# Order of VectorE's work in a two-layer encoder: gate sums held behind a split, spread additions, placed low parts, reordered row blocks

## The chip, the cores and the metric

The kernel runs on one core of a Trainium2 chip. The metric is the time on the device of one execution, in microseconds (us). The kernel is one program that goes through the whole model once. The five engines are called as in the profile: PE (TensorE, matmuls), PEld (its weight loads), DVE (VectorE), ACT (ScalarE), POOL (GpSimd), and SP (SyncE), which issues most of the DMA transfers. Each engine works through a list of instructions in a fixed order that is set when the program is built; an instruction starts when the one before it on its engine is done and the semaphores that it waits for have arrived.

## What is computed

The reference is an encoder of two layers on a sequence of 1024 rows of 1024 numbers, all float32. The first layer mixes by latent attention, the second by differential attention; both are chunk-causal.

```
for i in range(DEPTH):                       # 2 layers
    mix = mla(h) if i % 2 == 0 else diff(h)
    h = layernorm(ALPHA * h + mix, ...)
    h = layernorm(ALPHA * h + swiglu(h, w_gu[i], w_down[i]), ...)

swiglu(x) = (silu(gate) * up) @ w_down,      gate, up = split(x @ w_gu)
```

x is (1024, 1024), w_gu is (1024, 2 x 2816) and w_down is (2816, 1024). The change concerns only swiglu and the layer norm behind it (in the second layer).

## The kernel before

**Products of 2x2 blocks by seven.** Both matrix products of swiglu are done with seven block products instead of eight: sums and differences of blocks of the activations and of the weights are formed first, seven products ("1" to "7") are taken, and their results are added up. In the gate stage, a unit (n, pr) is product pr for block n of 22 weight blocks. Its weight side comes from `prepare` (line 573) and its matmuls from `consume` (line 602). The activation side is the operands t1, t2, t3, t4 and b22.

**Two parts for every operand.** PE multiplies in fp32r, so `split` (line 509) cuts every operand into a high part (an ACT cast) and a low part (a subtraction on DVE or POOL, line 511); a product then is three matmuls per 128 rows: high by high, high by low, low by high. One unit of the gate stage is 12 matmuls of 128x512. Tiles called op_* hold both parts of an operand.

**Gate stage.** Six weight blocks are begun ahead (`load_pre`): their products "1" and "2" run while the layer norm ahead still ends. Each load_pre takes a buffer tagged wr, of which there are two, for the raw weights gp, so that the load of gp n + 2 can be issued when the subtractions that read gp n are done. The raw blocks gr of the other units come in by load (line 564), and a gate sum (line 586, then 588 and 590) forms sums and differences in place in gr. The raw loads are 1 MB each for gr and 512 KB for gp, all on SP's queue.

**Down stage.** Four accumulators of one PSUM bank each serve one product, `whole` (line 865), 4 banks by 11 parts of the contraction. An activation part op_h comes from `from_h`, a weight part from a generator such as `t1` or `t4`. When a product is done, `added` (line 881) adds its four banks to rows of z on DVE, and the banks can be used again. The first product's 12 additions (line 921) stand in the program between it and the second. The last product of the last layer ("4") runs part by part on all four banks for parts 0 and 1, then on two banks for parts 2 to 10, then on the other two; its weight parts are called wt41_j, with low parts on POOL for j = 0 and 1 and on DVE for the others.

**What sets the order.** The program is written as a stream of operations; the build sorts them by priority and dependency into one order for each engine. `behind(i, j)` (line 167) adds a dependency without a semaphore between instructions, so that i is kept after j in that order. banks_read, h_lows and t4_lows are lists of instructions kept for that purpose: the additions that read banks, the low parts of the activation parts, and those of the last product's weight parts.

**The tail.** Behind the last product each of four row blocks goes through add (line 987), centred (998), scale (1003, with a power on POOL in 1004) and done (1009, followed by its store from SP in 1010). `on_v` chains these DVE instructions in written order.

## Time and profile before

| | us |
|---|---|
| median of 3 runs (lowest, highest) | 2276.8 (2276.53, 2277.06) |
| profiled execution | 2275.05 |
| its span, first to last instruction | 2273.3 |
| PE busy in the span | 2245.0 |
| DVE, ACT, POOL busy | 1550.6, 1016.7, 862.6 |
| mean granted clock of PE, share of full speed | 0.998 |

The profiled execution is 1.75 us longer than its span. Rows of the timeline read: start, length, engine, line, operation, output<-inputs, size, number of like instructions in a row, and in brackets the idle time of the engine before it with what ended it. Lengths of DVE instructions in a row overlap a little: the starts of 128x512 subtractions follow each other by 0.60 us, though each is listed with 0.68. Line numbers are those of the kernel before. Two names: the first number behind a tile's name is the layer (0 or 1), the last one counts buffers and can be passed over.

### The profile page before, as it was taken

Reading aid. Unit: us, or ns where it says so; the run is one execution under the profiler, and the core shown is the slowest. Engines: PE = TensorE matmul, PEld = TensorE weight load, DVE = VectorE, ACT = ScalarE, POOL = GpSimd, SP = SyncE. Lnnn points to the kernel's source line nnn. Section 1 sums busy time; section 2 is a strip of 40 time slices with the busy share of each in tenths; the row PEclk is TensorE's granted clock in tenths of the full one; section 3 lists DMA queues with packets and bytes.
Section 4 is the critical chain, followed back from the end, with each engine's and each line's share of the span. In section 5 each row is a group of like instructions: output and inputs, shape, how many; then the busy total and the mean of one; then the engine's idle time right before and its main releaser. Section 6 shows DMA issues by size and latency. Waiting matters only on the chain. (4 is left out here: it accounts for less than half of the span.)

```text
span 2273.3 us, 31157 instructions
## 1 busy us (share of the span) xinstructions
PE 2245.0 (99%) x11426; PEld 1914.2 (84%) x11426; DVE 1550.6 (68%) x2909; ACT 1016.7 (45%) x2101; POOL 862.6 (38%) x673
## 2 busy tenths in 40 slices
PE   9999999999999999999999999999999999999998
PEld 9898998888888888888888898987778888888886
DVE  6666665596656668778476667576587666668778
ACT  4465664352333334445465656555442333334443
POOL 2233452114444446555232424221014444446562
PEclk9999999999999999999999999999999999999999
DMA  5121325334313238554310212153344223247554
GB/s 206 41 97 59 119 98 186 139 140 140 126 70 139 70 126 323 196 179 167 107 47 23 67 38 70 26 208 116 125 153 152 94 98 111 96 156 271 181 179 149
DMA packets 104281, 289.33 MB, mean 127 GB/s; under 512 B 8640, under 2 KB 31808, under 8 KB 93632
## 3 DMA queue, kind: packets, MB, share of 16 engines
q1 hardware_dynamic: 100128, 277.90, 34.8%
q0 software_dynamic: 4000, 9.44, 1.5%
q8 instruction: 90, 1.47, 0.3%
q14 instruction: 63, 0.52, 0.1%
HBM read 205.78 MB, written 77.33 MB: 125 GB/s over the span
## 5 line engine op out<-in xcount | busy, mean ns | idle before, releaser
L511 ACT CAST op_g<-gr 128x512 fp32r<-128x512 f32 x240 | 147.5, 622 | 404.7 <-PE gb L555 225.2
L511 POOL TENSOR_TENSOR op_g<-gr,op_g 128x512 fp32r<-128x512 f32 x104 | 146.0, 1408 | 300.6 <-DVE tmp L649 160.5
L511 DVE TENSOR_TENSOR op_h<-rh,op_h 128x512 fp32r<-128x512 f32 x154 | 163.7, 1092 | 61.2 <-ACT op_h L511 61.1
L555 PE MATMUL ga<-xh_m,op_g 128*128 128x512 f32 x512 | 168.1, 389 | 0.0
L511 ACT CAST op_h<-rh 128x512 fp32r<-128x512 f32 x154 | 92.5, 619 | 145.8 <-DMA rh<-h_dr 39.4
L858 PE MATMUL dw<-op_w_t,op_h 128*128 128x512 f32 x660 | 151.9, 390 | 0.0
L858 PEld LDWEIGHTS dw<-op_w_t,op_h 128*128 128x128 f32 x660 | 123.3, 188 | 25.6
L232 ACT ACTIVATE l_b<-l_b,mx_b 128x256 f32<-128x256 f32 (+7 forms) x128 | 99.5, 778 | 75.9 <-DVE mx_b L229 74.0
L511 POOL TENSOR_TENSOR op_w_t<-tt,op_w_t 128x512 fp32r<-128x512 f32 x66 | 99.9, 1516 | 82.6 <-ACT op_w_t L511 78.1
L1440 POOL TENSOR_SCALAR l_b<-l_b,r_b,cst 128x128 f32<-128x128 f32 (+3 forms) x64 | 52.5, 821 | 204.8 <-DVE r_b L234 198.8
L858 PE MATMUL dx<-op_w_b,op_h 128*128 128x512 f32 x528 | 120.3, 389 | 0.0
L858 PEld LDWEIGHTS dx<-op_w_b,op_h 128*128 128x128 f32 x528 | 99.1, 188 | 20.6
L555 PE MATMUL gc<-t1h_f,op_g 128*128 128x512 f32 x352 | 116.2, 391 | 0.0
L555 PE MATMUL gb<-t4h_f,op_g 128*128 128x512 f32 x352 | 115.7, 390 | 0.5 <-DVE tmp L640 0.5
L511 DVE TENSOR_TENSOR op_g<-gr,op_g 128x512 fp32r<-128x512 f32 x136 | 110.2, 810 | 8.7 <-ACT op_g L511 8.2
L555 PE MATMUL gc<-b22h_f,op_g 128*128 128x512 f32 x352 | 115.5, 389 | 0.0
L555 PE MATMUL gb<-t3h_f,op_g 128*128 128x512 f32 x352 | 115.2, 389 | 0.0
L555 PE MATMUL gb<-t2h_f,op_g 128*128 128x512 f32 x352 | 115.1, 389 | 0.0
L511 POOL TENSOR_TENSOR op_g<-s,op_g 128x512 fp32r<-128x512 f32 x40 | 54.7, 1368 | 156.1 <-ACT op_g L511 156.0
L555 PEld LDWEIGHTS ga<-xh_m,op_g 128*128 128x128 f32 x512 | 96.1, 188 | 19.9
L155 PE MATMUL bp<-xT_f,h_wb 128*128 128x512 f32 x256 | 102.8, 402 | 0.0
L157 PE MATMUL bp<-xT_f,l_wb 128*128 128x512 f32 x256 | 101.6, 397 | 0.0
(389 smaller groups left out, 6738.4 us busy)
## 6 DMA issues: line engine op xcount, KB each, us to landing
gr<-in_w_gu SPq DMA_DIRECT2D x44, 1024.0 KB, 6.8
rh<-h_dr SPq DMA_DIRECT2D x28, 1024.0 KB, 5.2
h_dr<-sh SPq DMA_DIRECT2D x22, 1024.0 KB, 4.9
h_dr<-hp SPq DMA_DIRECT2D x22, 768.0 KB, 4.0
tt<-in_w_dn SPq DMA_DIRECT2D x22, 512.0 KB, 8.3
rh<-h_dr SPq DMA_DIRECT2D x14, 768.0 KB, 4.3
z<-xs_dr SPq DMA_DIRECT2D x16, 512.0 KB, 11.2
rw_b<-in_w_dn SPq DMA_DIRECT2D x8, 1024.0 KB, 8.8
```

Of the source, the lines that this page charges most:

```text
L155: T.matmul(ps_out, lh, rh, start=(i == 0), stop=False)
L157: T.matmul(ps_out, ll, rh, start=False, stop=(i == n - 1))
L232: newest["exp"] = A.activation(l[:, :n], l[:, :n], AF.Exp, bias=mx, scale=-1.0, accum_out=sm).ins
L511: return A.copy(hi, src).ins, eng.tensor_tensor(lo, src, f32(hi), ALU.subtract).ins
L555: T.matmul(o, w[:, a, kc], x[b][:, k, :], start=(first and k == 0 and (a, b) == (0, 0)), stop=(k == 3 and a == 1), skip_group_check=True,)
L858: i = T.matmul(o, h[:, a, c], w[:, b_], start=(first and (a, b_) == (0, 0)), stop=(last and a == 1), skip_group_check=True,).ins
L1440: G.tensor_scalar(l1[:, :n], l1[:, :n], r1, nlam, ALU.mult, ALU.mult)
```

## The change

There are four edits. First, in the gate stage, the gate sum for products "5" of weight blocks 0 and 1 is kept behind the low part of the fourth of the six early splits (`fourth`, of gp 3), and so are the parts of b22. Second, the 12 additions of the first down product are issued two at a time ahead of each of the first activation parts of the second product (`among`) instead of all ahead of it. Third, in the last product of the last layer the low parts of wt41_0 and wt41_1 go to DVE, and the low parts of activation parts 2 and later are kept behind the additions that read the banks (2 to 5) or behind the low parts of the weight part four places earlier (6 and later; before: from 8 on). Fourth, in the tail, done(1) is written behind scale(2), and done(3) is cut in three pieces of 512, 256 and 256 columns with a store each, where it was two of 512.

```diff
@@ -583,7 +583,9 @@
                     load(n + 2)
             a11, a12, a21, a22 = (r[n][:, i] for i in range(4))
             if pr == ("5" if n < 2 else "6"):
-                V.tensor_tensor(a21, a21, a22, ALU.add)
+                i = V.tensor_tensor(a21, a21, a22, ALU.add).ins
+                if n < 2:
+                    behind(i, fourth[1])
             if pr == ("3" if n < 2 else "6"):
                 V.tensor_tensor(a11, a21, a11, ALU.subtract)
             if pr == "3":
@@ -693,6 +695,7 @@
 
         for n in range(4):
             load_pre(n, G if n < 2 else V)
+        fourth = newest["op"]
         gates(0)
         load(0)
         load(1)
@@ -731,7 +734,7 @@
             part("t1", k, r12, V)
         load_pre(4, V)
         for k in range(4):
-            part("b22", k, r22, V)
+            part("b22", k, r22, V, fourth)
         load_pre(5, V)
         held = [newest["op"]]
         gates(4)
@@ -794,8 +797,8 @@
                             behind(i, k)
                         if j == 2 * early - 1:
                             activations(NFF - 1, *last_args, newest["op"])
-                    if name == "4" and next_x is None and j > 7:
-                        behind(newest["op"][1], t4_lows[j - 4])
+                    if name == "4" and next_x is None and j > 1:
+                        behind(newest["op"][1], banks_read[min(j - 6, -1)] if j < 6 else t4_lows[j - 4])
                     yield t
 
         def w_block(kh, cs, name):
@@ -847,7 +850,7 @@
                     yield unit(r, f"t4_{j}", G, ("o",))
                     continue
                 t = poolx.tile([P, 2, 512], F32R, tag=f"tt{j}", name=f"wt4{layer}_{j}")
-                cast, lo = split((t[:, 0], t[:, 1]), r, V if j > 1 else G)
+                cast, lo = split((t[:, 0], t[:, 1]), r, V)
                 t4_lows.append(lo)
                 newest["t4"] = cast, lo
                 yield t
@@ -918,12 +921,16 @@
         for tb in (4, 5, 6, 7, 0, 1, 2, 3):
             load_down(z[tb], x_src[tb * P:(tb + 1) * P, :])
             sums[tb] = small(f"fs{layer}_{tb}", 2)
-        for t in range(4):
-            added(0, hi_half, x4[t], t, None, ALPHA)
-            added(1, hi_half, x4[t], t, None, ALPHA)
-            added(1, lo_half, x4[t], t, None, ALPHA)
-
-        whole(y4, hs, t1(), True)
+        adds = [(t, a) for t in range(4) for a in ((0, hi_half), (1, hi_half), (1, lo_half))]
+
+        def among(hs):
+            for h in hs:
+                for t, (half, cs) in adds[:2]:
+                    added(half, cs, x4[t], t, None, ALPHA)
+                del adds[:2]
+                yield h
+
+        whole(y4, among(hs), t1(), True)
         for t in range(4):
             added(0, hi_half, y4[t], t)
             added(1, hi_half, y4[t], t)
@@ -1003,9 +1010,8 @@
                 on_v(V.tensor_scalar(ve, ssq[t][:, 0:1], e, LN_EPS, ALU.add, ALU.add))
                 G.tensor_tensor(rs[t], ve, mhalf[:, 0:1], ALU.pow)
 
-            def done(t, n=1):
-                for i in range(n):
-                    c = slice(i * D // n, (i + 1) * D // n)
+            def done(t, cuts=(0, D)):
+                for c in map(slice, cuts, cuts[1:]):
                     on_v(V.scalar_tensor_tensor(y[t][:, c], y[t][:, c], rs[t], b[:, c], ALU.mult, ALU.add))
                     nc.sync.dma_start(x_dst[t * P:(t + 1) * P, c], y[t][:, c])
 
@@ -1018,16 +1024,16 @@
             centred(1)
             scale(1)
             done(0)
-            done(1)
             add(2)
             centred(2)
             scale(2)
+            done(1)
             done(2)
             add(3)
             centred(3, 1)
             scale(3)
             centred(3, 0)
-            done(3, 2)
+            done(3, (0, D // 2, 3 * D // 4, D))
         else:
             gb = big_tile(f"gb_{nm}", F32)
             for i, src in enumerate((lng, lnb)):
```

How the edits move instructions on DVE, at three places of the second layer. First, the start of the gate stage, as it was. L511 is a low part: t1l of the operand t1, b22l of b22, op_gp of an early weight block; L586, L588 and L590 are the gate sums of the weight blocks gr1_0 and gr1_1:

```order
L511 TENSOR_TENSOR op_gp1_4_1_16501<-gp1_4_16499,op_gp1_4_1_16501 128x512
L586 TENSOR_TENSOR gr1_0_16409<-gr1_0_16409 128x512
L511 TENSOR_TENSOR t1l_f1_16483<-xr01_m1_15707,t1h_f1_16482 128x512
L588 TENSOR_TENSOR gr1_0_16409<-gr1_0_16409 128x512
L511 TENSOR_TENSOR t1l_f1_16483<-xr01_m1_15707,t1h_f1_16482 128x512 x3
L590 TENSOR_TENSOR gr1_0_16409<-gr1_0_16409 128x512
L586 TENSOR_TENSOR gr1_1_16411<-gr1_1_16411 128x512
L511 TENSOR_TENSOR b22l_f1_16485<-xr11_m1_15705,b22h_f1_16484 128x512 x4
L511 TENSOR_TENSOR op_gp1_3_2_16352<-gp1_3_16347,op_gp1_3_2_16352 128x512
L588 TENSOR_TENSOR gr1_1_16411<-gr1_1_16411 128x512
L725 TENSOR_TENSOR xr11_m1_15705<-xr11_m1_15705,xr01_m1_15707 128x512
L511 TENSOR_TENSOR op_gp1_4_2_16504<-gp1_4_16499,op_gp1_4_2_16504 128x512
```

And now; L588 and L590 of before are L590 and L592 of the changed kernel, and L725 is L728:

```order
L511 TENSOR_TENSOR op_gp1_4_1_16501<-gp1_4_16499,op_gp1_4_1_16501 128x512
L511 TENSOR_TENSOR t1l_f1_16483<-xr01_m1_15707,t1h_f1_16482 128x512 x4
L511 TENSOR_TENSOR op_gp1_3_2_16352<-gp1_3_16347,op_gp1_3_2_16352 128x512
L586 TENSOR_TENSOR gr1_0_16409<-gr1_0_16409 128x512
L511 TENSOR_TENSOR b22l_f1_16485<-xr11_m1_15705,b22h_f1_16484 128x512 x2
L586 TENSOR_TENSOR gr1_1_16411<-gr1_1_16411 128x512
L590 TENSOR_TENSOR gr1_0_16409<-gr1_0_16409 128x512
L511 TENSOR_TENSOR b22l_f1_16485<-xr11_m1_15705,b22h_f1_16484 128x512
L728 TENSOR_TENSOR xr11_m1_15705<-xr11_m1_15705,xr01_m1_15707 128x512
L511 TENSOR_TENSOR b22l_f1_16485<-xr11_m1_15705,b22h_f1_16484 128x512
L728 TENSOR_TENSOR xr11_m1_15705<-xr11_m1_15705,xr01_m1_15707 128x512
L590 TENSOR_TENSOR gr1_1_16411<-gr1_1_16411 128x512
```

The four t1l and op_gp1_3_2 now stand ahead of the first gate sum, and the parts of b22 stand behind them, between the gate sums.

Second, the start of the last product, as it was: L511 op_h is an activation part's low part, L193 ends a layer norm, L883 adds a finished bank dw to rows of z, and L841 forms a difference for a weight part:

```order
L511 TENSOR_TENSOR op_h1_4_0_20724<-rh1_4_0_20722,op_h1_4_0_20724 128x512
L511 TENSOR_TENSOR op_h1_4_1_20745<-rh1_4_0_20722,op_h1_4_1_20745 128x512
L511 TENSOR_TENSOR op_h1_4_2_20764<-rh1_4_0_20722,op_h1_4_2_20764 128x512
L511 TENSOR_TENSOR op_h1_4_3_20777<-rh1_4_0_20722,op_h1_4_3_20777 128x512
L193 SCALAR_TENSOR_TENSOR z1_7_19534<-z1_7_19534,rs_f1_7_20510,fb1_19537 128x1024
L511 TENSOR_TENSOR op_h1_4_4_20792<-rh1_4_1_20790,op_h1_4_4_20792 128x512
L511 TENSOR_TENSOR op_h1_4_5_20807<-rh1_4_1_20790,op_h1_4_5_20807 128x512
L511 TENSOR_TENSOR op_h1_4_6_20820<-rh1_4_1_20790,op_h1_4_6_20820 128x512
L511 TENSOR_TENSOR op_h1_4_7_20833<-rh1_4_1_20790,op_h1_4_7_20833 128x512
L883 SCALAR_TENSOR_TENSOR z1_0_19293,fs1_0_19553<-z1_0_19293,dw1_0_20004 128x512
L883 SCALAR_TENSOR_TENSOR z1_1_19294,fs1_1_19555<-z1_1_19294,dw1_1_20005 128x512
L883 SCALAR_TENSOR_TENSOR z1_2_19295,fs1_2_19557<-z1_2_19295,dw1_2_20006 128x512
```

And now (L883 is L886, L841 is L844):

```order
L511 TENSOR_TENSOR op_h1_4_0_20724<-rh1_4_0_20722,op_h1_4_0_20724 128x512
L511 TENSOR_TENSOR op_h1_4_1_20745<-rh1_4_0_20722,op_h1_4_1_20745 128x512
L511 TENSOR_TENSOR wt41_0_20730<-rw1_t4_0_20727,wt41_0_20730 128x512
L511 TENSOR_TENSOR wt41_1_20749<-rw1_t4_0_20727,wt41_1_20749 128x512
L193 SCALAR_TENSOR_TENSOR z1_7_19534<-z1_7_19534,rs_f1_7_20510,fb1_19537 128x1024
L886 SCALAR_TENSOR_TENSOR z1_0_19293,fs1_0_19553<-z1_0_19293,dw1_0_20004 128x512
L511 TENSOR_TENSOR op_h1_4_2_20764<-rh1_4_0_20722,op_h1_4_2_20764 128x512
L886 SCALAR_TENSOR_TENSOR z1_1_19294,fs1_1_19555<-z1_1_19294,dw1_1_20005 128x512
L511 TENSOR_TENSOR op_h1_4_3_20777<-rh1_4_0_20722,op_h1_4_3_20777 128x512
L886 SCALAR_TENSOR_TENSOR z1_2_19295,fs1_2_19557<-z1_2_19295,dw1_2_20006 128x512
L511 TENSOR_TENSOR op_h1_4_4_20792<-rh1_4_1_20790,op_h1_4_4_20792 128x512
L886 SCALAR_TENSOR_TENSOR z1_3_19296,fs1_3_19559<-z1_3_19296,dw1_3_20007 128x512
```

Two activation parts and the two weight parts stand ahead of the additions, and one more activation part between each two of them; the others follow later.

Third, the additions of the first down product (L886, dx) with what stands around them, in the changed kernel (L824 is a difference for a weight part of the second product):

```order
L824 TENSOR_TENSOR tt1_9_19291<-tt1_9_19291 128x512
L511 TENSOR_TENSOR op_h1_5_3_19620<-rh1_5_0_19539,op_h1_5_3_19620 128x512
L824 TENSOR_TENSOR tt1_10_19292<-tt1_10_19292 128x512
L886 SCALAR_TENSOR_TENSOR z1_4_19531<-z1_4_19531,dx1_0_19320 128x512
L886 SCALAR_TENSOR_TENSOR z1_5_19532<-z1_5_19532,dx1_1_19321 128x512
L886 SCALAR_TENSOR_TENSOR z1_6_19533<-z1_6_19533,dx1_2_19322 128x512
L886 SCALAR_TENSOR_TENSOR z1_7_19534<-z1_7_19534,dx1_3_19323 128x512
L886 SCALAR_TENSOR_TENSOR z1_0_19293<-z1_0_19293,dx1_0_19320 128x512 x2
L886 SCALAR_TENSOR_TENSOR z1_1_19294<-z1_1_19294,dx1_1_19321 128x512 x2
L886 SCALAR_TENSOR_TENSOR z1_2_19295<-z1_2_19295,dx1_2_19322 128x512 x2
L886 SCALAR_TENSOR_TENSOR z1_3_19296<-z1_3_19296,dx1_3_19323 128x512 x2
L511 TENSOR_TENSOR op_h1_5_4_19643<-rh1_5_1_19641,op_h1_5_4_19643 128x512
```

The additions are 12 in one piece, between tt1_10's difference and activation part 4. In the kernel before, the same instructions stand in the same order.

## The prediction

> **What bounds the kernel now.** I read the page first, then the waits of PE, then the timeline around each wait that the diff touches.
>
> ```profile
> PE 2245.0 (99%) x11426; PEld 1914.2 (84%) x11426; DVE 1550.6 (68%) x2909; ACT 1016.7 (45%) x2101; POOL 862.6 (38%) x673
> ```
>
> PE is busy for 2245.0 of a span of 2273.3 us. The number and shape of the matmuls of these products stay as they are, so the change can only win at three things: idle time of PE, matmuls at a lowered clock, and the stretch behind PE's last matmul. The waits view of PE (engine, line, tile, what was waited for: us in total, times, longest) names the idle places near the diff:
>
> ```profile
> PE dy L858 <- DVE op_h L511: 2.2, 2, 1.1
> PE ga L555 <- DVE op_gp L511: 1.9, 1, 1.9
> PE dw L858 <- DVE z L883: 1.5, 1, 1.5
> PE gb L555 <- DVE tmp L640: 0.5, 1, 0.5
> ```
>
> These are four targets: 2.2 us in the second down product (1.1 in each layer), 1.9 in the gate stage of one layer, 1.5 in the last product, 0.5 in the gate stage of the other layer. Together they are 6.1 us, or 0.27% of the run; about 0.2%, here 4.55 us, is what a measurement of this kernel can tell from no change.
>
> **The gate sums (fourth split).** Here lies most of it, because the wait costs twice:
>
> ```profile
> 1656.96 0.73 PE L555 MATMUL ga<-xh_m,op_gp 128*128 128x512 f32 x2 [1.94 <-DVE op_gp L511]
> ...
> 1656.00:1658.00 2.00, 1.04 (x5) 0.86 (x5) 2.00 (x4) 1.31 (x3) 0.00 (x0) 1.00 0.76 324
> 1658.00:1660.00 2.00, 2.00 (x7) 1.63 (x6) 2.00 (x5) 0.00 (x0) 0.00 (x0) 0.61 0.48 201
> 1660.00:1662.00 2.00, 2.00 (x6) 1.52 (x6) 2.00 (x4) 1.62 (x4) 0.00 (x0) 0.53 0.54 160
> ```
>
> In the windows, the numbers behind the length are the busy times of PE, its weight loads, DVE, ACT and POOL, then the granted clock. PE stands for 1.94 us, and right behind it the granted clock is 0.61 and 0.53 for two windows: work lost is 0.39 x 2 + 0.47 x 2 = 1.7 us. With the 0.15 us by which the first matmul's start is late beyond the shown idle, this place costs 1.94 + 0.15 + 1.7 = 3.8 us. Why is the low part of op_gp1_5_1 late?
>
> ```profile
> 1640.56 0.69 DVE L586 TENSOR_TENSOR gr<-gr 128x512 f32<-128x512 f32 x1 [3.93 <-DMA gr<-in_w_gu]
> 1645.38 2.49 DVE L511 TENSOR_TENSOR b22l_f<-xr_m,b22h_f 128x512 fp32r<-128x512 f32 x4
> 1647.79 0.68 DVE L511 TENSOR_TENSOR op_gp<-gp,op_gp 128x512 fp32r<-128x512 f32 x1
> 1656.23 0.68 DVE L511 TENSOR_TENSOR op_gp<-gp,op_gp 128x512 fp32r<-128x512 f32 x1
> ...
> 1636.29 2.18 ACT L511 CAST t1h_f<-xr_m 128x512 fp32r<-128x512 f32 x4
> 1652.12 0.62 ACT L511 CAST op_gp<-gp 128x512 fp32r<-128x512 f32 x1 [0.58 <-DMA gp<-in_w_gu]
> ...
> 1648.50 0.33 SPq L570 DMA_DIRECT2D gp<-in_w_gu  x1
> ```
>
> Read backwards: PE waits for the subtraction at 1656.23; its cast ran at 1652.12, as soon as the load landed; that load was issued at 1648.50, 3.6 us earlier, when op_gp1_3_2 (1647.79) had freed its buffer; and op_gp1_3_2 stood behind a gate sum (L586) for which DVE idled 3.93 us, behind four t1l and four b22l subtractions, which were ready earlier. The change puts the four t1l and op_gp1_3_2 ahead of that gate sum.
>
> By the same rows: the t1h casts end at 1636.29 + 2.18 = 1638.47, so the fourth t1l ends at about 1639.2 (0.6 each, by the rows' pitch), op_gp1_3_2 at 1639.8, and the load is issued at 1639.9 and lands 3.6 later, at 1643.5. In the new order 14 instructions of 0.60, the gate sum at 1640.56 the first, run ahead of op_gp1_5_1, so this subtraction runs at 1640.56 + 8.4 = 1649.0 to 1649.7 instead of 1656.23. PE asks for it at about 1654: 4 us to spare, also if the load took twice its 3.6. The wait and the clock's drop go, -3.8; so does a smaller one at 1650.88, where PE waits for op_gp1_3_2 itself:
>
> ```profile
> 1650.39 0.39 PE L555 MATMUL ga<-xl_m,op_gp 128*128 128x512 f32 x1
> 1650.88 0.50 PE L555 MATMUL ga<-xh_m,op_gp 128*128 128x512 f32 x1
> 1651.21 0.39 PE L555 MATMUL ga<-xl_m,op_gp 128*128 128x512 f32 x1
> 1651.44 0.62 PE L555 MATMUL ga<-xh_m,op_gp 128*128 128x512 f32 x2
> ```
>
> The starts step by 0.49 and 0.33 where 0.23 is the pitch of the next: 0.36. Sum -4.15, bounds -4.15 and 0 (another unit of the same queue takes the wait over). What is now queued behind: the gate sums of gr1_0 and gr1_1 come 1 to 3 instructions later against the operands that they feed, and the units that use them (gc1_0, gc1_1) have 2 us and more by the same count of 0.6 us per instruction.
>
> The same edit in the other layer finds no such stall to remove:
>
> ```profile
> 498.64 0.67 DVE L640 TENSOR_TENSOR tmp<-pg,gb 128x512 f32<-128x512 f32 x1
> 499.37 0.51 PE L555 MATMUL gb<-t4h_f,op_g 128*128 128x512 f32 x1 [0.51 <-DVE tmp L640]
> ```
>
> There the gate sum's data landed early, and holding it lets DVE idle until the t1h cast; everything behind is some 0.9 to 1.4 us later by the count, within slacks of 2 us and more except at this one place, where 0.5 becomes about 0.7: +0.2 (bounds -0.3, +0.5).
>
> [...] The trace speaks for the wait: the drop begins 1.5 us behind this longest of the waits (1656.96, and the clock is 1.00 in the window up to 1658), and behind the wait of 1.07 that is shown next the clock stays at 1.00:
>
> ```profile
> 2096.06:2101.34 5.28, 5.28 (x23) 4.40 (x24) 3.56 (x6) 1.14 (x2) 2.25 (x1) 1.00 0.48 149
> ```
>
> **The additions of the first down product** are meant to be spread among activation parts. But in the instruction order as built all 12 still stand in one block between the same neighbours on DVE, in both layers, as before:
>
> ```profile
> 2088.16 7.25 DVE L883 SCALAR_TENSOR_TENSOR z<-z,dx 128x512 f32<-128x512 f32 x12
> 2095.33 4.29 DVE L511 TENSOR_TENSOR op_h<-rh,op_h 128x512 fp32r<-128x512 f32 x7
> ...
> 2096.06 5.28 PE L858 MATMUL dy<-op_w_t,op_h 128*128 128x512 f32 x22 [1.07 <-DVE op_h L511]
> ```
>
> So the block of 7.25 us still delays the next activation part past PE's need, and both waits of 1.1 stay: 0. If they went, it would be worth 2.2 and up to 0.25 of late start at each (0.15 at the gate stage's wait), so -2.7.
>
> **The last product.**
>
> ```profile
> 2225.85 4.57 DVE L511 TENSOR_TENSOR op_h<-rh,op_h 128x512 fp32r<-128x512 f32 x4
> 2231.54 2.48 DVE L511 TENSOR_TENSOR op_h<-rh,op_h 128x512 fp32r<-128x512 f32 x4
> 2233.95 0.67 DVE L883 SCALAR_TENSOR_TENSOR z<-z,dw 128x512 f32<-128x512 f32 x1
> ...
> 2224.74 3.93 POOL L511 TENSOR_TENSOR wt<-rw_t,wt 128x512 fp32r<-128x512 f32 x2 [2.42 <-ACT wt L511]
> ...
> 2221.79 11.49 PE L858 MATMUL dw<-op_w_t,op_h 128*128 128x512 f32 x50
> 2234.78 17.51 PE L858 MATMUL dw<-wt,op_h 128*128 128x512 f32 x76 [1.49 <-DVE z L883]
> ```
>
> The old product ends at 2221.79 + 11.49 = 2233.28, and PE waits until 2234.78 for z1_0's addition, which reads the bank that PE will overwrite. The addition stands behind eight op_h subtractions, the first four at 1.14 us each while POOL subtracts beside them, the other four at 0.60. Now the two POOL subtractions (3.93) come to DVE (2 x 0.60) and only two op_h go first, so z1_0's addition runs as soon as its bank is done, about 2229.5, and the fourth right behind 2233.3. PE goes on at once: -1.5.
>
> The price: the op_h of parts 2 to 10 are now done while PE consumes them. DVE has three instructions a part (op_h, wt, the difference), 1.81 us, and PE six matmuls a part, 1.36. Adding up the queue from 2233.9, the operand of part 2 is ready 2.1 us ahead of need, and the lead shrinks by 0.45 a part: it is nothing at part 6, -0.2 at part 7, and grows again from part 9, where op_h no longer follow. I take +0.2; bounds -1.65 (with PE's start-up at the wait) and +0.8 net. Past SP's queue: the third rh load waits for the buffer that op_h1_4_3 frees, about 1.5 us later than before:
>
> ```profile
> 2235.85 1.67 ACT L511 CAST op_h<-rh 128x512 fp32r<-128x512 f32 x3 [6.82 <-DMA rh<-h_dr]
> ```
>
> Landing at about 2237.4 instead of 2235.85 it is ahead of op_h1_4_8's place near 2242, but behind its three casts (1.67) ACT has the cast of wt part 4, done at 2239.6, just when DVE wants it. Net -1.3.
>
> **The tail.**
>
> ```profile
> 2258.25 2.48 DVE L1009 SCALAR_TENSOR_TENSOR y_f<-y_f,rs_f,fb 128x1024 f32<-128x1024 f32 x2 [0.32 <-POOL rs_f L1004]
> 2260.64 0.68 DVE L987 SCALAR_TENSOR_TENSOR z<-z,dw 128x512 f32<-128x512 f32 x1
> 2264.07 1.28 DVE L1009 SCALAR_TENSOR_TENSOR y_f<-y_f,rs_f,fb 128x1024 f32<-128x1024 f32 x1 [0.66 <-POOL rs_f L1004]
> 2265.27 0.68 DVE L987 SCALAR_TENSOR_TENSOR z<-z,dw 128x512 f32<-128x512 f32 x1
> ...
> 2254.62 10.36 PE L858 MATMUL dw<-wt,op_h 128*128 128x512 f32 x45
> ...
> out_dram<-y_f SPq DMA_DIRECT2D x3, 512.0 KB, 2.6
> out_dram<-y_f SPq DMA_DIRECT2D x2, 256.0 KB, 2.0
> ```
>
> PE ends at 2264.98, and the last addition starts at 2265.27. One L1009 (1.24) moved behind scale(2) fills the 0.66 in which DVE waits for POOL, so the addition starts when PE is done: -0.25. The last store is 128 KB, and 256 KB less took 0.6 less: -0.3. One more issue on SP and one more DVE start may cost 0.05: net -0.5, bounds 0 and -0.9. All else that the order moves (some heads' transposes and stores) has slacks of 2 to 4 us: 0 +- 0.3.
>
> **Sum.** -4.15 + 0.2 + 0 - 1.3 - 0.5 = -5.75. The profiled execution took 2275.05, 1.75 outside its span and 1.75 below the median of the runs; it becomes 2269.3, and the median 2276.8 becomes **2271.0** (-0.25%). Its own range, 2269.5 to 2272.5.
>
> **The rivals.**
> The additions do spread: 2271.0 - 2.7 = 2268.3. The block in the built order speaks against it; 0.03.
> [...]
> The wait moves to the next unit of the same DVE queue with its own drop: +3.8, 2274.8; for it speaks that the gate sums are only re-sorted, not less; 0.11.
> The last product becomes bound by DVE, 0.45 a part from part 6 to 10: +2.2, 2273.2; 1.81 against 1.36 speaks for it, the lead of 2 us against; 0.13.
> Slower: in the first layer, DVE idles at the front of the gate queue for the t1h cast. If its delay there exceeds the slacks of about 2 us, units with t1 and b22 wait, each above 1.9 us drawing the half clock: 3.8 a place. At one place it eats the gain (2274.8), at three it is 2271.0 + 11.4 = 2282.4. The count of 0.9 to 1.4 us speaks against; 0.04.
> Forecast: 0.61.
>
> **How the numbers follow.** Faster by over 0.2% is below 2272.2: nearly all of the forecast (0.58), the spread, 0.03, and the milder half of the next two (0.06): 0.67. Slower: the last, 0.04. Within 0.2%: 0.29. The range goes from 2268.0 (tail and last product at their bounds, or the additions spread) to 2275.2 (the wait moved).
>
> **What would show it.** Gone should be the waits of ga for op_gp and of dw for z, and the granted clock 1.00 in every window of the gate stage; dy's 2.2 us for op_h should still be there, and gb's for tmp about 0.7. The subtraction ahead of ga1_5 should run near 1649. In the last product no wait above 0.3 us; the last store 128 KB, at 1.7 us. A ga, gc or gb wait of 1 us or more in either gate stage, or waits of dw for wt that add to more than 1 us, would make the prediction wrong.

## The result, and the profile after

| | us |
|---|---|
| kernel before, 22 runs (lowest, highest) | 2277.05 (2275.25, 2279.12) |
| changed kernel, 22 runs (lowest, highest) | 2273.65 (2271.16, 2277.9) |
| ratio, 95% interval | 0.9985, 0.9979 to 0.9991 |
| profiled execution after, its span | 2272.51, 2270.7 |

The change gains 3.4 us, 0.15%; with 22 runs of each the interval excludes no change. The forecast was 5.75 us. The time lies 1.15 us above the forecast's own range. It lies within the wide range only because that reaches up to 2275.2 for the rival in which the wait moves. The gain is within 0.2%, where the prediction gave the larger chance to more than 0.2%.

What PE now waits for near the diff (waits view of PE in the changed kernel: us in total, times, longest):

```profile
PE dy L861 <- DVE op_h L511: 2.6, 2, 1.5
PE gb L555 <- DVE tmp L642: 1.0, 2, 0.8
PE gb L555 <- ACT op_g L511: 0.7, 1, 0.7
```

The waits of ga for op_gp and of dw for z are gone, and dy's for op_h are still there, as forecast. But the waits of gb have grown from 0.5 to 1.69 us, and this is where a part of the gain went.

**Second layer's gate stage.** Timeline of the changed kernel, DVE and PE:

```profile
1651.96 0.68 DVE L511 TENSOR_TENSOR op_gp<-gp,op_gp 128x512 fp32r<-128x512 f32 x1
...
1655.82 0.62 PE L555 MATMUL ga<-xh_m,op_gp 128*128 128x512 f32 x2
...
1679.61 0.69 DVE L586 TENSOR_TENSOR gr<-gr 128x512 f32<-128x512 f32 x1 [0.92 <-DMA gr<-in_w_gu]
...
1683.02 0.89 PE L555 MATMUL gb<-t3h_f,op_g 128*128 128x512 f32 x2
...
1686.64 0.50 PE L555 MATMUL gb<-t4h_f,op_g 128*128 128x512 f32 x1 [0.19 <-DVE tmp L642]
```

The low part of op_gp1_5_1 is made at 1651.96. The whole execution runs 2.48 us later here than the one before did, so this is 1649.5 on its clock, within the 1649.0 to 1649.7 forecast. PE begins this operand's unit 3.4 us after its end without a wait, and the granted clock stays at 1.00:

```profile
1656.00:1658.00 2.00, 2.00 (x10) 1.65 (x10) 2.00 (x5) 1.91 (x4) 0.00 (x0) 1.00 0.46 197
1658.00:1660.00 2.00, 2.00 (x11) 1.65 (x10) 2.00 (x5) 1.04 (x2) 0.00 (x0) 1.00 0.78 328
1660.00:1662.00 2.00, 2.00 (x11) 1.65 (x10) 2.00 (x4) 0.96 (x3) 0.00 (x0) 1.00 0.48 70
```

Some 27 us later two small waits appear that the kernel before did not have: one of 0.04 inside the group at 1683.02 (0.89 for two matmuls where 0.62 is usual) and one of 0.19 at 1686.64. A gate sum that waits 0.92 us for its load stands ahead of them on DVE.

**First layer's gate stage.** Two timelines: first DVE in the kernel before, then DVE, POOL and PE in the changed one, whose line numbers are 2 higher (L638 was L636, L590 was L588, L592 was L590):

```profile
493.47 0.68 DVE L588 TENSOR_TENSOR gr<-gr 128x512 f32<-128x512 f32 x1
...
494.67 0.68 DVE L636 TENSOR_TENSOR tmp<-pg,gb 128x512 f32<-128x512 f32 x1
495.27 0.80 DVE L590 TENSOR_TENSOR gr<-gr 128x512 f32<-128x512 f32 x1
```

```profile
495.07 1.72 DVE L590 TENSOR_TENSOR gr<-gr 128x512 f32<-128x512 f32 x1
496.71 0.68 DVE L638 TENSOR_TENSOR tmp<-pg,gb 128x512 f32<-128x512 f32 x1
...
497.90 1.53 DVE L592 TENSOR_TENSOR gr<-gr 128x512 f32<-128x512 f32 x1
...
494.94 1.29 POOL L511 TENSOR_TENSOR op_g<-s,op_g 128x512 fp32r<-128x512 f32 x1 [46.33 <-ACT op_g L511]
...
497.53 0.47 PE L555 MATMUL gb<-t3h_f,op_g 128*128 128x512 f32 x1 [0.67 <-ACT op_g L511]
501.29 0.50 PE L555 MATMUL gb<-t4h_f,op_g 128*128 128x512 f32 x1 [0.79 <-DVE tmp L642]
```

The addition L638 of block 1 (tmp0_1) reads the bank that PE wants to go on with. In both kernels it stands behind a subtraction for weight block 4 (gr0_4: L588 at 493.47 before, L590 at 495.07 now). Before, this took 0.68 us; now it takes 1.72, while POOL subtracts beside it from 494.94 on. Three sums and differences of blocks 3 and 4, which before came ahead of block 0's addition, now also stand between the two additions. From the start of the stage, tmp0_1's addition runs 1.3 us later than before. PE starts 0.14 us after this addition's end, so it is the addition that releases it, though the row names the cast. Where one wait of 0.51 stood, there are now 0.67 and 0.79.

**Last product.** Timeline of the changed kernel, PE and DVE:

```profile
2219.69 12.63 PE L861 MATMUL dw<-op_w_t,op_h 128*128 128x512 f32 x55
2232.16 4.02 PE L861 MATMUL dw<-wt,op_h 128*128 128x512 f32 x17
...
2243.94 1.97 PE L861 MATMUL dw<-wt,op_h 128*128 128x512 f32 x7
...
2229.01 0.68 DVE L886 SCALAR_TENSOR_TENSOR z<-z,dw 128x512 f32<-128x512 f32 x1
...
2247.44 0.69 DVE L511 TENSOR_TENSOR wt<-rw_t,wt 128x512 fp32r<-128x512 f32 x1
```

The first addition runs at 2229.01 (forecast about 2229.5), PE passes from the old product to the new without a stop, and the waits view names no later wait. But at part 7 PE is held up by 0.2 us: the seven matmuls at 2243.94 take 1.97 us where 1.75 is usual, and the one that comes late starts at 2244.95, 0.06 us behind the end of this part's subtraction on DVE. DVE has the last weight part at 2248.1, 14 us before PE's end.

**Tail.** Timeline, then the stores with their size and median time from issue to landing:

```profile
2262.55 0.68 DVE L994 SCALAR_TENSOR_TENSOR z<-z,dw 128x512 f32<-128x512 f32 x1
...
2265.88 1.54 DVE L1015 SCALAR_TENSOR_TENSOR y_f<-y_f,rs_f,fb 128x512 f32<-128x512 f32 x3 [0.44 <-POOL rs_f L1011]
```

```profile
out_dram<-y_f SPq DMA_DIRECT2D x1, 256.0 KB, 2.0
out_dram<-y_f SPq DMA_DIRECT2D x2, 128.0 KB, 2.0
```

PE ends at 2262.48, and the last addition follows at once (forecast). But a store of 128 KB takes 2.0 us like one of 256 KB, and three pieces take DVE 1.54 us where two took 1.41 (2268.59, L1009, before). From PE's end to the end of the span: 8.32 us before, 8.22 now. In three kernels further down, which keep the moved done(1) but store the last block in two halves, it is 8.10 to 8.12 (e6, e7, e10): the move gains 0.2, and the third piece takes 0.1 of it back.

**By stretches.** Each length is a difference of two starts of PE in the trace. First layer: from the first matmul with op_gp0_2_1 to the first of product 5 of block 2. Second layer: the same, from op_gp1_2_2. Last product: from the start of the product ahead of it (dw1_0 with op_h1_6_0) to PE's end.

| stretch | before | after | difference | forecast |
|---|---|---|---|---|
| first layer's gate stage | 47.09 | 48.24 | +1.15 | +0.2 |
| second layer's gate stage | 42.78 | 39.35 | -3.43 | -4.15 |
| last product | 121.64 | 120.08 | -1.56 | -1.3 |
| tail | 8.32 | 8.22 | -0.10 | -0.5 |
| sum | | | -3.94 | -5.75 |

The medians differ by 3.4, the two profiled executions by 2.54. In the latter, 0.42 more is the first layer's dy wait (1.50 where it was 1.08; it is 1.08 again in e1, e9 and others), and 0.72 lies ahead of the first gate stage, where nothing was changed: over all profiled executions here that stage begins at 443.3 (before) to 446.9 us. Each stretch, like each stage length below, is measured in one execution.

### The profile page after: what moved, and what is told of

It reads as the page before. It is cut to its first block, busy times and chain, and to the rows that moved or that the text cites. A ratio compares the mean times of both kernels' runs of the same rounds, so it can differ in the third digit from the quotient of the medians.

```text
span 2270.7 us, 31160 instructions
## 1 busy us (share of the span) xinstructions
PE 2243.8 (99%) x11426; PEld 1912.6 (84%) x11426; DVE 1552.5 (68%) x2912; ACT 1017.7 (45%) x2101; POOL 863.7 (38%) x671
## 4 chain that ended last, share of the span: by engine, by line
PE 87%; DVE 6%; issue 2%; ACT 2%; DMA 2%; POOL 0%; SPq 0%; POOLq 0%; DVEq 0%; ACTq 0%
PE gb L555 15%; PE gc L555 10%; PE ga L555 10%; PE dw L861 7%; PE s_a L226 4%; PE dv L861 3%; PE dx L861 3%; PE s_b L226 3%; PE bp L156 3%; PE bp L155 3%; PE bp L157 3%; PE zp_a L430 3%; PE o_a L265 2%; PE o_b L265 2%; PE dy L861 2%
## 5 line engine op out<-in xcount | busy, mean ns | idle before, releaser
L511 ACT CAST op_g<-gr 128x512 fp32r<-128x512 f32 x240 | 147.5, 622 | 402.9 <-PE gb L555 223.7
L511 POOL TENSOR_TENSOR op_g<-gr,op_g 128x512 fp32r<-128x512 f32 x104 | 146.0, 1408 | 299.5 <-DVE tmp L651 160.4
L511 DVE TENSOR_TENSOR op_h<-rh,op_h 128x512 fp32r<-128x512 f32 x154 | 167.3, 1113 | 59.6 <-ACT op_h L511 59.4
L511 ACT CAST op_h<-rh 128x512 fp32r<-128x512 f32 x154 | 92.7, 619 | 141.8 <-DMA rh<-h_dr 44.4
L861 PEld LDWEIGHTS dw<-op_w_t,op_h 128*128 128x128 f32 x660 | 123.3, 188 | 25.8 <-DVE op_h L511 0.5
L511 POOL TENSOR_TENSOR op_w_t<-tt,op_w_t 128x512 fp32r<-128x512 f32 x66 | 100.1, 1520 | 82.1 <-ACT op_w_t L511 82.1
L511 DVE TENSOR_TENSOR op_g<-gr,op_g 128x512 fp32r<-128x512 f32 x136 | 109.5, 805 | 8.8 <-ACT op_g L511 8.4
L511 POOL TENSOR_TENSOR op_g<-s,op_g 128x512 fp32r<-128x512 f32 x40 | 55.7, 1391 | 151.6 <-ACT op_g L511 151.6
```

Of the source, the lines that this page charges most:

```text
L511: return A.copy(hi, src).ins, eng.tensor_tensor(lo, src, f32(hi), ALU.subtract).ins
L861: i = T.matmul(o, h[:, a, c], w[:, b_], start=(first and (a, b_) == (0, 0)), stop=(last and a == 1), skip_group_check=True,).ins
```

## The experiments

Unless said otherwise a kernel is compared with the kernel before. Ratios have their 95% interval.

**e1, e2: the gate edit alone, in both layers and in the second only.** The diff is that of e2; in e1 the two conditions on the layer are not there.

```diff
-                V.tensor_tensor(a21, a21, a22, ALU.add)
+                i = V.tensor_tensor(a21, a21, a22, ALU.add).ins
+                if n < 2 and layer == 1:
+                    behind(i, fourth[1])
...
+        fourth = newest["op"]
...
-            part("b22", k, r22, V)
+            part("b22", k, r22, V, fourth if layer == 1 else ())
```

> The kernel before with the gate edit alone (gate sums and parts of b22 behind the fourth split, in both layers). Theory: it carries both the gain and the hidden loss of the change. In the second layer the wait of 1.9 us and the lowered clock go and about 0.5 us of new waits comes in front of the products 7 and 4 of block 1 and 0: -3.4. In the first layer two waits of gb, of 0.7 and 0.8 us, replace the one of 0.5: +1.1. So about -2.3 us in all. Rival: the first layer's two waits were a matter of that one execution and not of the edit; then gb waits about 0.5 us there as before, and the time is about -3.4 us.

> The gate edit in the second layer only; in the first layer VectorE's order is that of the kernel before. Theory (the first layer's loss belongs to the edit): the first layer shows one wait of gb of about 0.5 us, the second none of ga; -3.4 us, 1.1 better than the edit in both layers. Rival (the first layer's loss is not of the edit): the same time as the edit in both layers, within its interval.

e1: 2276.33 against 2277.57, ratio 0.9995 (0.9986 to 1.0004). e2: 2276.53, 0.9996 (0.9987 to 1.0005), and so not the 1.1 better than e1 that was expected. The first layer's stage is 48.24 in e1, as in the changed kernel, and 47.06 in e2: the loss there belongs to the edit. The second layer's is 40.44 in e1 but 42.69 in e2: with the ga wait gone in both, e2 keeps nothing of it. Where it went (timeline of e2; PE, DVE, ACT and SP):

```profile
1686.62 0.76 PE L555 MATMUL gb<-t3h_f,op_g 128*128 128x512 f32 x1 [2.51 <-ACT tmp L665]
...
1685.80 0.67 DVE L638 TENSOR_TENSOR tmp<-pg,gb 128x512 f32<-128x512 f32 x1
...
1681.69 0.69 DVE L586 TENSOR_TENSOR gr<-gr 128x512 f32<-128x512 f32 x1 [1.05 <-DMA gr<-in_w_gu]
...
1669.72 2.19 ACT L511 CAST t4h_f<-xr_m 128x512 fp32r<-128x512 f32 x4 [2.75 <-DVE t3l_f L511]
1671.82 0.58 ACT L618 ACTIVATE pg<-ga 128x512 f32<-128x512 f32 x1
...
1672.42 0.33 SPq L694 DMA_DIRECT2D pg_dr<-pg  x1
1676.66 0.33 SPq L564 DMA_DIRECT2D gr<-in_w_gu  x1
```

Read backwards, this is a second chain of waits: PE waits for tmp1_1's addition (1685.80; PE starts 0.14 or 0.15 us after its end at this wait in e1 to e6); that stands five places behind the gate sum of gr1_4, for whose load DVE idles 1.05 us; the load is issued 4.2 us after the store of pg; the store follows the activation at 1671.82, and this stands on ACT behind four casts that wait for DVE. Once PE no longer stops at ga, it arrives early here. So what the edit keeps in the second layer is decided by this chain. Counted from the stage's start, the load is issued at 24.5 us in the changed kernel, 24.9 in e1 and 25.8 in e2, and PE's wait at this place is 0.04, 1.31 and 2.51. Why the same edit issues it at different times was not followed up.

**e3: only the parts of b22 behind the fourth split, the gate sums free.**

```diff
+        fourth = newest["op"]
...
-            part("b22", k, r22, V)
+            part("b22", k, r22, V, fourth if True else ())
```

> Only half of the gate edit: the parts of b22 behind the fourth split, the gate sums left as they were. In the order, op_gp1_3_2 then still stands behind the gate sum that waits for its load, but ahead of the b22 parts. Theory A (the delay by the b22 parts and the other work is what made the load late): op_gp1_3_2 runs near 1645.4 instead of 1647.8 on the clock of before, op_gp1_5_1 near 1651 to 1653, ahead of PE's need at 1654.9: no ga wait, clock 1.00, -3.8 us and nothing lost in the first layer, whose order is unchanged. Theory B (the idle 3.9 us behind the gate sum is what counts): the wait shrinks but stays above 0.5 us, and the gain is 2.5 us or less.

2279.01 against 2277.57, ratio 1.0008 (1.0000 to 1.0017). The ga wait goes in this kernel too, so the place of the b22 parts is enough to remove it; but a gb wait of 2.94 us takes its place, and the stage is 42.66 long.

**e4: the additions of the first down product really spread, in both layers.**

```diff
-        whole(y4, hs, t1(), True)
+        def take(n, low=None):
+            for t, (half, cs) in adds[:n]:
+                added(half, cs, x4[t], t, None, ALPHA)
+                if low is not None:
+                    behind(banks_read[-1], low)
+            del adds[:n]
+
+        def among(hs):
+            for j, h in enumerate(hs):
+                if j >= 4:
+                    take(2, newest["op"][1])
+                yield h
+
+        take(6)
+        whole(y4, among(hs), t1(), True)
```

> The kernel before with the additions of the first down product really spread: six ahead of activation part 4 of the second product and two each behind the low parts of parts 4, 5 and 6, held there by order dependencies. Theory (the block of 7.25 us is what makes part 4 late): part 4 is ready 3.6 us earlier, both waits of dy for op_h go, -2.7 us, with no new wait, since the parts then come every 1.8 us against PE's need of 2.7. Rival (part 4 is late by its load or its cast): the waits stay above 0.5 us each and the time changes by less than 1 us.

2276.23, 0.9996 (0.9987 to 1.0005). Both dy waits are gone, but in the second layer two waits of dw for activation parts come in their place, 0.18 and 1.91 us. There DVE waits for a load of rw_t that is issued at 2153.02 where it was 2149.95 before; why was not followed up. From the timeline of PE:

```profile
2165.74 0.50 PE L858 MATMUL dw<-op_w_t,op_h 128*128 128x512 f32 x1 [1.91 <-DVE op_h L511]
...
1658.13 0.73 PE L555 MATMUL ga<-xh_m,op_gp 128*128 128x512 f32 x2 [1.94 <-DVE op_gp L511]
```

The last row is a chance find in the part that e4 leaves as it was: the same wait of 1.94 us as before, but the granted clock stays at 1.00 behind it (windows):

```profile
1658.00:1660.00 2.00, 1.87 (x8) 1.57 (x9) 2.00 (x5) 0.37 (x1) 0.00 (x0) 1.00 1.08 455
1660.00:1662.00 2.00, 2.00 (x11) 1.65 (x10) 2.00 (x4) 1.11 (x2) 0.00 (x0) 1.00 0.49 70
```

The stage is 43.10 long all the same, as a gb wait of 1.56 follows. So the lowered clock is no sure price of that wait, and its absence alone gains nothing here.

**e5, e6, e7: the activation ahead of the casts.** To bring gr1_4's load forward, e5 keeps the four t4 casts behind the last activation of the early blocks, on top of the change. e6 has this and the gate edit in the second layer only, with the change's last product and tail (block 3 in two pieces); e7 adds the spread of e4 in the first layer only.

```diff
-                    A.activation(g0, acc[n, "a"], AF.Silu)
+                    newest["silu"] = A.activation(g0, acc[n, "a"], AF.Silu).ins
...
-            part("t4", k, r21, V)
+            part("t4", k, r21, V, (newest["silu"],))
```

> The changed kernel, with one more order dependency: ScalarE's four casts of t4 stay behind the last activation of the early blocks (the one that writes pg1_4). Theory (second chain): in the second layer that activation, the store of pg1_4 behind it and the load of gr1_4 into the freed buffer set when the gate sum of gr1_4 runs; this sum heads VectorE's queue ahead of the addition that frees the bank that PE wants, and so it takes back part of the gain. In the kernel before, the activation ran 22.1 us behind PE's first matmul of ga1_2 with its second operand, right when PE was done; in the changed one at 19.7, though PE was done at 17.2. Now it should run near 17.4, the gate sum of gr1_4 near 27.5 instead of 29.5 to 29.9, and the waits of gb in the second layer (0.2 to 1.3 us) go: 0.5 to 1.3 us faster than the changed kernel. Rival (the waits of gb come from the order of VectorE's own work): they stay.

> What the theory says is worth keeping: the gate edit in the second layer only, with the casts of t4 behind that activation, the last product's edit, and of the tail only done(1) behind scale(2), with the last row block in two pieces as before; the additions as before. Theory: the first layer keeps its one wait of 0.5 us; second layer -3.9, last product -1.6, tail -0.2: -5.7 us against before, about 2 us faster than the change. Rival (first layer's loss or second chain misread): not faster than the change.

> The kernel of the run ahead, and the additions of the first down product really spread, in the first layer only. Theory: the wait of dy for op_h of 1.1 us goes in the first layer with nothing in its place there; -1.2 us more, so -6.9 us against before. Rival (the additions' place is paid for elsewhere in the first layer too): no faster than the run ahead.

e5: 2277.51 against 2278.04, 0.9997 (0.9988 to 1.0006), by the medians worse than the change alone. The stage in the second layer is 43.51 us long, with a gb wait of 3.10 us. e6: 2276.61, 0.9997 (0.9988 to 1.0006), gb waits of 0.73 and 2.54. e7: 2275.25, 0.9991 (0.9982 to 1.0000); the first layer's dy wait is gone with nothing in its place. Both stay some 4 us short of what was expected of them. The idea of e5 failed on the transfers (SP's queue in e5):

```profile
1668.01 0.33 SPq L564 DMA_DIRECT2D gr<-in_w_gu  x1
1668.82 0.33 SPq L694 DMA_DIRECT2D pg_dr<-pg  x1
1677.40 0.33 SPq L564 DMA_DIRECT2D gr<-in_w_gu  x1
```

The store now starts 0.8 us behind the load of gr1_3 (three such loads of 1 MB took 4.9 us from issue to landing in the kernel before, by the median), so that both run at once, and the next load, which needs the stored buffer, is issued 8.6 us after the store and not 4.2: earlier in, later out.

**e8: longer idle time, on purpose.** Three (first layer) and six (second) extra DVE instructions behind the additions, each the maximum of half a row block of z with itself, and activation part 4 kept behind them (this line is not shown).

```diff
+        last = banks_read[-1]
+        for _ in range((3, 6)[layer]):
+            i = V.tensor_tensor(z[3][:, lo_half], z[3][:, lo_half], z[3][:, lo_half], ALU.max).ins
+            behind(i, last)
+            last = i
```

> The kernel before with VectorE instructions added behind the additions of the first down product: each takes the maximum of a half row of z with itself, which changes nothing. Three in the first layer and six in the second, so that PE's waits of 1.1 us there become about 2.9 and 4.7 us. It tells what length of a wait draws the lowered clock. Theory of the prediction (a wait of 1.9 us is enough): the clock is halved for some 3.4 us behind both waits, 1.7 us more each. Rival (the drop behind the 1.9 us wait was chance: in the run with the spread additions the same wait of 1.94 us was followed by none): none behind the wait of 2.9, one behind 4.7 at most.

2289.91 in one run, against 2278.04. The dy waits became 3.25 and 7.00 us, longer than expected, and the granted clock falls to 0.50 at each. It is taken up in the last section.

**e9, e12: the gate sum held behind the additions, on the change and on the kernel before.**

```diff
                 if n < 2:
                     behind(i, fourth[1])
+                elif n in (4,):
+                    behind(i, newest["u3"])
...
-                V.tensor_tensor(u3, p1, acc[n, "b"], ALU.add)
+                newest["u3"] = V.tensor_tensor(u3, p1, acc[n, "b"], ALU.add).ins
```

> The changed kernel, with one edit more: the gate sum of weight block n = 4 (L586) is held on DVE's queue behind the last addition of the first-half products of output block 1, in both layers, so that its wait for the load no longer stands ahead of the additions which free the banks that PE wants. Theory (a second chain: load of block 4 -> gate sum at the head of DVE's queue -> the additions behind it -> PE's bank): the waits of 0.67 and 0.79 us in the first layer's gate stage and the waits of 0.04 and 0.19 us (up to 1.3 in the run of the gate edit alone) in the second layer's go, 1.3 to 2.5 us less than the changed kernel: 2271 to 2272.5 us where the changed one has 2273.65. Rival 1: the additions are late because of slow instructions beside GpSimd, whatever their order: the waits stay at 0.5 us and more each, and the time is the changed kernel's within 0.5 us. Rival 2: the held sum makes block 4's own parts late: PE waits at the first product with block 4 for 1 us or more, 2274 us or more.

> The kernel before with the hold of e9 alone: the gate sum of weight block n = 4 behind the additions of block 1's first-half products, in both layers; everything else as before. Theory (two waits in a row in the second layer, the one of ga for op_gp and the one of gb for the additions; the hold alone removes only the second): in the first layer the wait of 0.51 us goes, with 0.16 us of late start; in the second the wait of 1.94 us and the lowered clock stay, since they lie 20 us ahead of the held sum: 0.5 to 0.9 us less than the kernel before, 2276.9 to 2277.3. Rival: one chain carries both waits, the hold alone brings what it brought to the changed kernel, 2.3 us or more: 2275.5 or less.

e9: 2271.09 against 2277.82, ratio 0.9967 (0.9955 to 0.9980). e12: 2275.84 against 2277.04, 0.9994 (0.9985 to 1.0003). In e9 the waits view of PE names no ga, gb or gc any more; of the lines of the diff only this one is left:

```profile
PE dy L863 <- DVE op_h L511: 2.2, 2, 1.1
```

Its DVE in the first layer (timeline; L640 is the addition, L642 and L644 the next ones):

```profile
493.34 0.68 DVE L511 TENSOR_TENSOR op_g<-gr,op_g 128x512 fp32r<-128x512 f32 x1
493.94 0.68 DVE L642 TENSOR_TENSOR tmp<-tmp,gc 128x512 f32<-128x512 f32 x1
494.54 0.68 DVE L640 TENSOR_TENSOR tmp<-pg,gb 128x512 f32<-128x512 f32 x1
```

The addition runs at 494.54, 2.2 us earlier than in the changed kernel at the same start of the stage. The stages of the runs side by side:

| kernel | first layer | second layer |
|---|---|---|
| before | 47.09 | 42.78 |
| hold alone (e12) | 46.24 | 42.56 |
| gate edit alone (e1) | 48.24 | 40.44 |
| gate edit in the second layer alone (e2) | 47.06 | 42.69 |
| the change | 48.24 | 39.35 |
| the change and the hold (e9) | 46.24 | 38.53 |

In the second layer the hold alone gains 0.22, the gate edit without it 0.1 to 3.43 (e2, e1, the change), both 4.25: two waits in a row, and the second one takes back what the first one's removal leaves. That it is the place of the sum on DVE's queue which counts, and not the time of its load, shows in e9: the load of gr1_4 is issued 25.9 us behind the stage's start, as late as in e2 (25.8), and PE does not wait. In the first layer the hold takes 0.85 from the kernel before, and 2.0 from the changed one. e9's own last product is 1.35 shorter than before and its tail 0.1, so that its stretches add up to 0.85 + 4.25 + 1.35 + 0.1 = 6.55 us; the medians differ by 6.7. (The two profiled executions differ by 5.66, as e9's first gate stage begins 0.79 later.) Against the change the hold gains 2.6 by the medians, though the ends of the two intervals touch.

**e10: e9 with the additions spread in the first layer only, and the last block stored in two halves.** The edit is e4's, with `if j >= 4 and layer == 0` and `take(6 if layer == 0 else 12)`, and `done(3, (0, D // 2, D))`.

> e9 with two edits more: the additions ahead of the second product's activation parts are spread among the parts in the first layer alone (6 ahead of the part, 2 each behind parts 4, 5 and 6), and the last block is stored in two halves, not three pieces. Theory: the first layer's dy wait of 1.1 to 1.5 us goes as it did when the additions were spread, nothing takes its place, and the stores cost the same: 1.0 to 1.5 us less than e9, 2269.5 to 2271.5 us. Rival: the order of the first layer's gate stage or of the second product is upset by the other, and the time is e9's within 0.5 us.

2269.91 against 2277.82, ratio 0.9962 (0.9949 to 0.9976), the best kernel of this study: 7.9 us less than before, 1.2 less than e9, though the intervals of these two overlap. Its waits view has one dy wait left, that of the second layer, and its timeline shows the additions apart:

```profile
901.41 3.66 DVE L888 SCALAR_TENSOR_TENSOR z<-z,dx 128x512 f32<-128x512 f32 x6
...
905.15 1.19 DVE L511 TENSOR_TENSOR op_h<-rh,op_h 128x512 fp32r<-128x512 f32 x1
906.25 1.27 DVE L888 SCALAR_TENSOR_TENSOR z<-z,dx 128x512 f32<-128x512 f32 x2
907.45 1.66 DVE L511 TENSOR_TENSOR op_h<-rh,op_h 128x512 fp32r<-128x512 f32 x1
```

**e11: the last product alone.**

```diff
-                    if name == "4" and next_x is None and j > 7:
-                        behind(newest["op"][1], t4_lows[j - 4])
+                    if name == "4" and next_x is None and j > 1:
+                        behind(newest["op"][1], banks_read[min(j - 6, -1)] if j < 6 else t4_lows[j - 4])
...
-                cast, lo = split((t[:, 0], t[:, 1]), r, V if j > 1 else G)
+                cast, lo = split((t[:, 0], t[:, 1]), r, V)
```

> The kernel before with the change's last product and its closing row blocks alone (low parts on DVE and placed, block 1's store moved, block 3's in three pieces); gates and additions as before. Theory: the wait of 1.49 us in the last product goes and nothing takes its place, and the tail gains about 0.1: 1.5 to 1.8 us less than the kernel before, about 2275.4. Rival: the last product's wait is taken up by the low parts that DVE now makes, and by the row blocks that wait for it: under 0.7 us less.

2276.66 against 2277.82, 0.9994 (0.9985 to 1.0003). The interval holds no change, so it is the trace that decides: the wait of dw for z is gone, no wait takes its place, and the stretch of the last product is 120.12 (before 121.64). What was expected names the moved store and the three pieces as well, but the kernel that ran has only the two edits shown: its closing row blocks are those of before, and so is its tail (8.3). The tail's edit was run only together with others.

## Why the prediction was right or wrong

**The ga wait (right).** The chain from the gate sum through op_gp1_3_2 and its buffer's load to op_gp1_5_1 was read rightly, to half a us. "The wait and the clock's drop go" came true in the changed kernel.

**The second layer's sum of -4.15 (size, too much in the change by 0.7).** What was removable measured 4.25, in e9. The change itself keeps 3.43, and kernels with the same edit keep 2.34 (e1) and 0.1 (e2). The step that failed is to book the removed wait in full without following PE to the next thing it needs: tmp1_1's bank, some 27 us later, behind gr1_4's gate sum and its load. That this load is late was to be seen in the timeline of before:

```profile
1680.71 0.69 DVE L586 TENSOR_TENSOR gr<-gr 128x512 f32<-128x512 f32 x1 [0.25 <-DMA gr<-in_w_gu]
```

DVE waits 0.25 us for it there, though PE comes about 4 us later than it does without the ga wait. This is the rival "the wait moves to the next unit of the same DVE queue" in kind, though it had the place wrong and its full price (+3.8) comes about only in e2, e3, e5, e6 and e7. That the change keeps as much as 3.43 is luck as far as the working goes: by e1 and e2 it hangs on when that load is issued.

**The clock's 1.7 (right in that execution, no constant).** e4's wait of 1.94 us without a drop shows that it is not the price of such a wait in every run. To a drop with another cause than this wait the forecast gave 0.08 (2272.7). No run shows such a cause near the edits: every lowered stretch in the windows there has an idle time of PE of 1.94 us or more ahead of its end. But such an idle time does not bring one every time, as the last section shows.

**The first layer's +0.2 (failed; +1.15, outside its bounds of -0.3 and +0.5).** The step that failed is "within slacks of 2 us and more except at this one place". I moved the queue as a whole by 0.9 to 1.4 us. In fact tmp0_1's addition, some 40 us behind the start of the stage, had no such slack: the order between the additions changed as well, and the subtraction for weight block 4 ahead of it, now beside POOL's, takes 1.72 us where it took 0.68. That the sums of block 4 ahead of the additions are what costs is shown by e9 and e12, where they are held and both kernels' gb waits go. The prediction followed the order at the start of the stage and not as far as the additions. The rival "slower" named this layer, but for t1 and b22, which waited nowhere.

**The additions (right).** They were not spread, and both dy waits stayed. Spreading them would not have been worth the -2.7 that I put on it: e4's second product is 1.4 us shorter in each layer (29.7 where it was 31.1), but its last product is 2.7 longer with the dw waits. In the first layer alone the spread is worth 1.4 us by that stretch, 1.2 by the medians of e10 and e9.

**The last product (right; -1.56 for -1.3).** The price of +0.2 came where it was put: at part 7 two matmuls start 0.32 and 0.34 us behind the ones ahead where 0.23 is the pitch. The rival "bound by DVE" did not come. The gain is larger because the wait cost 1.7 us in full, with PE's late start behind it; the sum had 1.5, and only the bound of -1.65 counted the start.

**The tail (failed in size; -0.1 for -0.5).** The earlier addition came as worked out: it starts 0.07 us behind PE's end where it was 0.29. The step that failed is the term "256 KB less took 0.6 less", carried on to 128 KB: both sizes land in 2.0 us. The two shorter pieces also cost DVE 0.13 more (1.54 for 1.41); the 0.05 for one more issue and one more start was an estimate with no row behind it.

## What to carry to other kernels

When a wait is removed, follow the waiting engine to the next operand or bank on its way and ask when that becomes ready; a saving can be booked only up to there. After an edit of priorities, compare the whole order of the stage and not only the place of the edit: look for long or waiting instructions (a sum that waits for a load) that now stand ahead of an addition which frees a bank. Keep such a sum behind the additions: on DVE's queue it is not its own work that costs, but what stands behind it.

## What was not expected of the hardware

**In these runs, idle times of PE of like length did and did not lower its granted clock.** Idle times of 1 us and more near the edits, with the clock in the windows, or the pitch of the matmuls, behind them: at 1.07, 1.08 and 1.49 us (kernel before) and 1.50 (changed kernel) it stayed at 1.00. At 1.31 (e1) and 1.56 (e4) the matmuls behind follow each other by 0.23 us, the usual pitch. From 1.91 to 2.94 us it fell to 0.50 in four cases (1.94 in the kernel before, 2.51 in e2, 2.54 in e6, 2.69 in e7) and stayed at 1.00 in three (1.91 and 1.94 in e4, 2.94 in e3). At 3.25 and 7.00 (e8) it fell to 0.50; at 3.10 (e5) the matmuls from 1688.61 to 1691.6 follow each other by 0.42 to 0.43 us. The windows of e8 around its idle time of 7.00 us, which begins at 2102.36 (the clock stands behind the five engines):

```profile
2104.00:2105.00 1.00, 0.00 (x0) 0.00 (x0) 0.94 (x2) 0.00 (x0) 0.00 (x0) 1.00 0.00 0
2105.00:2106.00 1.00, 0.00 (x0) 0.00 (x0) 0.99 (x2) 0.00 (x0) 0.00 (x0) 0.85 0.00 0
...
2110.00:2111.00 1.00, 1.00 (x4) 0.81 (x3) 0.51 (x1) 0.00 (x0) 0.00 (x0) 0.50 0.75 106
2111.00:2112.00 1.00, 1.00 (x4) 0.81 (x3) 0.00 (x0) 0.48 (x1) 0.00 (x0) 0.50 0.75 311
2112.00:2113.00 1.00, 1.00 (x5) 0.73 (x4) 0.69 (x1) 0.66 (x2) 0.27 (x1) 0.73 1.02 434
```

With the 0.50 of the windows between, 0.85 means lowered for 0.30 of its window, from 2105.70, and 0.73 means up to 2112.54: 6.84 us, of which 3.18 us lie behind the restart. The same sum for the windows of the kernel before,

```profile
1658.00:1659.00 1.00, 1.00 (x5) 0.82 (x4) 1.00 (x3) 0.00 (x0) 0.00 (x0) 0.73 0.95 401
...
1661.00:1662.00 1.00, 1.00 (x4) 0.81 (x3) 1.00 (x3) 1.00 (x3) 0.00 (x0) 0.56 0.68 246
```

gives 1658.46 to 1661.88, 3.42 us, just half of it. In e2 the windows read 0.56, 0.50, 0.50 and 0.73 from 1686 to 1690, which is 3.42 us again, from 1686.12 to 1689.54. The stretch does not always begin at the same distance from the idle time: 1.50 us behind PE's restart in the kernel before (1656.96) and 1.02 behind it in e6 (1687.78, restart at 1686.76), but 0.50 ahead of it in e2 (restart at 1686.62) and 3.66 ahead of it at the 7.00 us of e8 (restart at 2109.36). What sets where it begins, and why 1.94 us lowered the clock in one execution and 1.94 and 2.94 us in two others did not, these runs do not show.

**The store of pg beside a load.** From the store's issue to that of the load behind it, 8.6 us pass in e5, where the store is issued 0.8 us behind the load of gr1_3; 5.4 in the kernel before, where it is 2.6 us behind it; 4.2 in e2, where it is 3.3. In these three runs, the sooner the store came behind the load of gr1_3, the longer the load that needs the stored buffer had to wait.
